# Attention steps between dense products, issued in runs of one kind and head

## The chip, the cores and the metric

The kernel runs on one core of a Trainium2 chip. The metric is the device time of one execution in microseconds (us); the output is compared with the reference. A core has TensorE (PE, matmuls; its weight loads, PEld, overlap them), VectorE (DVE), ScalarE (ACT), GpSimd (POOL), SyncE (SP, which here issues transfers) and 16 DMA engines.

## The reference

One layer of a decoder trunk: 512 tokens, 1024 features, 16 heads of 64, all in float32.

```python
hn = rms_norm(x, norm_g)
proj = hn @ w_in                      # queries, keys, values; six forget logits; gates of the FoX heads
q, k = rms_norm(q, q_gain), rms_norm(k, k_gain)          # per head
o_moba = moba_attention(...)          # heads 0-3: linear position bias; two blocks of 256, so all past keys
o_fox = forgetting_attention(...)     # heads 4-9: logits plus a cumulated log-sigmoid of the forget logits
o_dil = dilated_attention(...)        # heads 10-15: three dilated windows, mixed by their denominators
y = concatenate([rms_norm(o_moba, g), rms_norm(o_fox, g) * sigmoid(gate), rms_norm(o_dil, g)])
x = x + y @ w_out
x = x + square(relu(rms_norm(x, mlp_norm) @ w_up)) @ w_down
```

All attention is causal softmax attention over 512 keys with a bias that differs by kind of head.

## The kernel before

**Dense products.** Every float32 operand is split into two float32r parts, high and low, and a product is three matmuls (high by high, high by low, low by high) into one of four accumulator banks ("acc"). `Stream` loads weight pieces [128, n] with SyncE's queue and splits them: ScalarE writes the high part (L95 or L98), VectorE the low part (L96 or L99), two pieces ahead of their use. `product` yields after each triple of matmuls (L202).

**The phases.** First the input projection in nine chunks, tokens on the output's partitions: queries and keys of four heads (512 columns), their values (256; 262 for the third, with the forget logits), and so on, at last the gates (384). Each has eight pieces for each of four token tiles, 32 triples. Then the output projection with features on the partitions, in four parts: first the row tiles of the MoBA and dilated heads for both halves of the columns (`OUT_ORDER[:2]`, 20 triples each), then those of the FoX heads (12 each). Then the MLP. Heads are worked on in the order MoBA, dilated, FoX; "head 15" below is the last in this order, and heads 10 to 15 are FoX.

**Attention in steps.** While the dense triples of the input projection and of the first two parts of the output projection are issued, steps of attention are put between them. All steps write to four further banks ("m"), which are used in turn; a step can't begin before what the step four banks earlier wrote has been read.

- `stack` (two a head; L423): four transposes that put queries, then keys, with features on the partitions; ScalarE copies them out (L425), and behind the keys two DMAs on ScalarE's queue (L429, L430) make a copy of them with both parts changed over ("stk2").
- `s` (four a head, one for each query tile; L442): two matmuls of 128 to 512 columns, the second with the changed-over keys; FoX heads add a mask (L447). VectorE adds the bias and finds the minimum (L454), ScalarE takes the exponential (L456).
- `pt` (three a head; L469): four, three and three transposes of the probabilities, split by ScalarE (L475) and VectorE (L476).
- `av` (two a head, four matmuls each, one bank for both; L493): probabilities times values; ScalarE copies the result (L498).
- `o` (one a head; L508): four transposes, VectorE's sum (L510) and GpSimd's division (L517). After the last head of a group, `group_norm` follows: ScalarE's squares (L533), a root on VectorE, and the scaling (L540 with the gate, or L544).
- `y` (four a group; L550): transposes of a group's result, split by ScalarE (L553) and VectorE (L554); the output projection reads all four.
- `root`, `norm` (normalisation of queries and keys) and `sig` (the gates' sigmoid) have no work on TensorE; `f` accumulates the forget logits.

**Who goes when.** TensorE's instructions run in program order, and this order comes from a small planner. Each step names the steps it needs and a lag for each (`LAG`, in us of the planner's own clock, which counts a full triple as 0.654 and a step by `COST`). After each triple `attend` adds to a credit (1.2 for 512 columns, in proportion for fewer; 2.75 in the output projection; never over 3.0). As long as the credit is at least 1.0, the first step in the list (oldest head first) all of whose needs are old enough is issued; it costs 1.0 of credit, or 0.25 if it has no work on TensorE. At the start of the output projection `attend_until` issues, without regard to credit or lags, what is still owed of the dilated heads up to their last `o`, and then the four `y` of their group (`y1`). Just then the buffers of the input projection are given up, and four loads of 512 KB fetch the residual into that space on SyncE's queue (L651). Before the third part of the output projection the four `y` of the FoX heads (`y2`) must be done.

Of the kernel before, what the change touches and what calls it, by code (L numbers as in the profile page):

```python
# [27 lines left out]
BIG = 1.0e30  # L28
# [6 lines left out]
# Heads in the order in which they are worked on: MoBA, dilated, FoX. A group is its range in that  # L35
# order and the first row tile of its part of the output projection.
# [4 lines left out]
# Column chunks of the input projection, in the order in which they are computed.  # L41
# [5 lines left out]
def chunk_columns(kind, i):  # L47
    """Columns (first, how many) of four heads' queries and keys, of four heads' values (FoX's
    forget logits behind the third), or of FoX's output gates."""
    if kind == "qk":  # L50
        return [(m * D + DH * h, DH) for m in range(2) for h in HEADS[4 * i : 4 * i + 4]]
    if kind == "v":
        forget = [(3 * D, NFOX)] if i == 2 else []
        return [(2 * D + DH * h, DH) for h in HEADS[4 * i : 4 * i + 4]] + forget
    return [(3 * D + NFOX, NFOX * DH)]


class Stream:
    """Weights as [128, n] pieces: raw from DRAM, then split into two float32r parts whose sum is
    the float32 weight (times a per-row gain where one is given)."""  # L60
# [51 lines left out]
def hymba_block(ctx: ExitStack, tc: tile.TileContext, a, out):  # L112
# [4 lines left out]
    small = ctx.enter_context(tc.tile_pool(name="small", bufs=2))  # L117
# [15 lines left out]
    pieces, in_first = [], []  # L133

    def group(first, size, alone=0):
        """Pieces from `first` on that follow one another in DRAM are loaded together, up to `size`."""
        i = first + alone
        while i < len(pieces):
            n = 1
            while n < size and i + n < len(pieces) and pieces[i + n][1] == pieces[i][1] + n:  # L140
                n += 1
            pieces[i][2] = n
            i += n
# [31 lines left out]
    def product(first, ks, operands, banks_n, done, G=2):  # L175
        """One chunk: four accumulators over the pieces `ks`, three passes for each product of
        split operands. Yields after each (piece, accumulator)."""
# [7 lines left out]
        if first == 0:  # L185
            # The very first piece: one pass over all accumulators after another, as parts arrive.
            wh, wl = w.take(0)
            acc = [bank("acc") for _ in range(banks_n)]
            for m in (0, 2, 1):
                for b in range(banks_n):  # L190
                    pairs, view = operands(ks[0], b, wh, wl)
                    lhs, rhs = pairs[m]
                    nc.tensor.matmul(view(acc[b]), lhsT=lhs, rhs=rhs, start=(m == 0), stop=False)
            order = [(k, b) for k, b in order if k > 0]
# [14 lines left out]
    def rsqrt(y, v, n, t=None):  # L209
        """y = v ** -0.5 for positive v: a first guess from the exponent's bits, then Newton."""  # L210
# [17 lines left out]
    # the first use of ScalarE's tables, before there is data to wait for  # L228
    warm = small.tile([P, 1], F32, name="warm", bufs=1)
    nc.scalar.activation(warm, ones[:, :1], AF.Ln)  # L230
    # and TensorE's clock, which only a busy TensorE raises
# [13 lines left out]
    for k in range(NK):  # L245
# [9 lines left out]
        # Sum of squares over this core's rows of features, one column for each token.  # L255
# [15 lines left out]
    # mean(x^2) + eps for each token, eps times that, and the reciprocal root.  # L271
# [102 lines left out]
    def forget():  # L374
        # log sigmoid(f) = min(f, 0) - log(1 + exp(-|f|))
# [18 lines left out]
    def gate():  # L394
        # ScalarE changes its tables for this one: behind the last exponentials
        tc.keep_in_program_order(nc.scalar.activation(gsig, gsig, AF.Sigmoid))

# [16 lines left out]
    def stack_step(h, which):  # L414
        def f():
# [10 lines left out]
            if which == 1:  # L426
                # the same keys with their two parts changed over
# [33 lines left out]
    # Blocks (key tile, query tile) of the transposed probabilities, by accumulator bank.  # L461
# [95 lines left out]
    # A step goes between two dense products once what it needs was issued long enough before it  # L557
    # (microseconds of TensorE's work), the oldest head first, so that TensorE does not wait.
    LAG = {"qk": 2, "root": 3, "zero": 0.0, "each": 2.5, "v": 2.5, "f": 5, "stack": 5.5, "s": 3.5, "pt": 3, "av": 3, "free": 1, "cum": 7, "norm": 9}
    COST = {"stack": 0.25, "s": 0.3, "pt": 0.4, "av": 0.6, "o": 0.43, "y": 0.22, "f": 0.43, "root": 0.0, "norm": 0.0, "sig": 0.0}  # L560
    steps = []
# [54 lines left out]
    def attend(rate, cost):  # L616
        """After a dense product that holds TensorE for `cost`: attention steps, at most `rate` each."""
# [3 lines left out]
        while credit >= 1.0:  # L621
# [3 lines left out]
            issue(s)  # L625
            credit -= 1.0 if COST[s[0][0]] else WEIGHT

# [80 lines left out]
    p2.close()  # L708

    def x2_stats():  # L710
        # each row the same: the reciprocal root mean square of every token
# [54 lines left out]
def bias_tables():  # L766
    """Minus the position terms of the logits of the ALiBi heads, which depend on shapes alone:
    slope * distance, minus the log of how many dilated branches hold the key, BIG where none does.
    Column u of row p is the distance p + 384 - u."""
# [13 lines left out]
def tiles_of(m, width):  # L783
    """[rows, columns] as [column chunk][row in tile][row tile][column]."""
# [38 lines left out]
```

## Time and profile before

| | |
|---|---|
| median of three runs | 650.38 us (650.24 to 651.02) |
| span of the profiled execution, first to last instruction | 649.9 us |
| TensorE busy in it | 640.5 us |
| VectorE busy | 385.4 us |
| ScalarE busy | 299.1 us |
| GpSimd busy | 91.6 us |
| DMA | 68.40 MB |

The profiled execution's own time is known as its span; the runs were timed without a profile, and their median lies 0.5 us over it. Busy time of TensorE counts pipelined matmuls by modelled ends, so a matmul's real cost is read from one start to the next, or from the pieces of the chain of waits, which don't overlap.

### The profile page before, as it was taken

Reading aid. Unit: us, or ns where it says so; the run is one execution under the profiler, and the core shown is the slowest. Engines: PE = TensorE matmul, PEld = TensorE weight load, DVE = VectorE, ACT = ScalarE, POOL = GpSimd, SP = SyncE. Lnnn points to the kernel's source line nnn. Section 1 sums busy time; section 2 is a strip of 40 time slices with the busy share of each in tenths; the row PEclk is TensorE's granted clock in tenths of the full one; section 3 lists DMA queues with packets and bytes.
Section 4 is the critical chain, followed back from the end, with each engine's and each line's share of the span. In section 5 each row is a group of like instructions: output and inputs, shape, how many; then the busy total and the mean of one; then the engine's idle time right before and its main releaser. Section 6 shows DMA issues by size and latency. Waiting matters only on the chain.

```text
span 649.9 us, 9018 instructions
## 1 busy us (share of the span) xinstructions
PE 640.5 (99%) x3294; PEld 544.1 (84%) x3294; DVE 385.4 (59%) x771; ACT 299.1 (46%) x615; POOL 91.6 (14%) x97
## 2 busy tenths in 40 slices
PE   8999999999999999999999999999999999999997
PEld 6798898898899988887888888888888888888886
DVE  6794696796598646778954544266324544433531
ACT  7467776776777666454332322233222333223310
POOL 4300210111020100024220200022000211000100
PEclk9999999999999999999999999999999999999999
DMA  8435234244322551223133332233323233223311
GB/s 305 149 97 148 81 93 106 81 137 122 84 62 87 153 189 40 97 98 119 44 130 99 97 97 98 97 98 96 99 97 98 73 122 98 97 91 105 94 68 66
DMA packets 24044, 68.40 MB, mean 105 GB/s; under 512 B 3114, under 2 KB 4666, under 8 KB 24000
## 3 DMA queue, kind: packets, MB, share of 16 engines
q1 hardware_dynamic: 18224, 57.84, 27.3%
q10 hardware_dynamic: 4432, 5.77, 3.8%
q0 software_dynamic: 1344, 4.22, 2.5%
q8 instruction: 26, 0.43, 0.3%
q14 instruction: 18, 0.15, 0.1%
HBM read 61.51 MB, written 2.11 MB: 98 GB/s over the span
## 4 chain that ended last, share of the span: by engine, by line
PE 90%; DVE 4%; DMA 3%; ACT 1%; issue 1%; SPq 0%; POOL 0%; ACTq 0%; DVEq 0%
PE acc L202 80%; PE m L442 3%; PE m L493 2%; PE m L469 2%; DMA wraw<-in_w_in 2%; PE m L423 1%; DMA stk<-stk 1%; DVE ptl L476 1%; PE m L508 1%; DVE wlo L96 1%; PE m L550 0%; DVE osum L510 0%; DVE m L454 0%; ACT xh L250 0%; DVE qksq L261 0%
## 5 line engine op out<-in xcount | busy, mean ns | idle before, releaser
L96 DVE TENSOR_TENSOR wlo<-wraw,whi 128x512 fp32r<-128x512 f32 (+3 forms) x136 | 85.4, 634 | 93.0 <-ACT whi L95 90.4
L95 ACT CAST whi<-wraw 128x512 fp32r<-128x512 f32 (+3 forms) x135 | 75.5, 567 | 121.7 <-PE acc L202 117.6
L98 ACT ACTIVATE whi<-wraw,gains 128x512 fp32r<-128x512 f32 x80 | 57.2, 724 | 101.2 <-PE acc L202 101.2
L202 PE MATMUL acc<-whi,xh 128*128 128x512 f32 (+3 forms) x284 | 103.5, 365 | 0.3 <-DVE vs L358 0.2
L99 DVE SCALAR_TENSOR_TENSOR wlo<-wraw,gains,whi 128x512 fp32r<-128x512 f32 x80 | 61.0, 774 | 70.1 <-ACT whi L98 70.0
L202 PE MATMUL acc<-zh,whi 128*128 128x512 f32 x256 | 100.8, 394 | 0.7 <-issue 0.7
L202 PE MATMUL acc<-hl,whi 128*128 128x512 f32 x256 | 100.9, 394 | 0.0
L202 PE MATMUL acc<-zl,whi 128*128 128x512 f32 x256 | 100.8, 394 | 0.0
L202 PE MATMUL acc<-hh,whi 128*128 128x512 f32 x256 | 100.4, 392 | 0.0
L202 PE MATMUL acc<-zh,wlo 128*128 128x512 f32 x256 | 99.4, 388 | 0.0
L202 PE MATMUL acc<-hh,wlo 128*128 128x512 f32 x256 | 99.3, 388 | 0.0
L202 PE MATMUL acc<-wlo,xh 128*128 128x512 f32 (+3 forms) x284 | 95.5, 336 | 0.5 <-DVE wlo L96 0.5
L202 PE MATMUL acc<-whi,xl 128*128 128x512 f32 (+3 forms) x284 | 95.7, 337 | 0.0
L731 POOL TENSOR_TENSOR sq<-relu 128x512 f32<-128x512 f32 x32 | 38.2, 1196 | 267.0 <-DVE relu L729 266.2
L202 PEld LDWEIGHTS acc<-zh,whi 128*128 128x128 f32 x256 | 48.1, 188 | 12.5 <-issue 1.3
L202 PEld LDWEIGHTS acc<-whi,xl 128*128 128x128 f32 x284 | 53.6, 189 | 5.2
L202 PEld LDWEIGHTS acc<-hh,whi 128*128 128x128 f32 x256 | 48.1, 188 | 11.2
L202 PEld LDWEIGHTS acc<-hh,wlo 128*128 128x128 f32 x256 | 48.1, 188 | 10.8
L202 PEld LDWEIGHTS acc<-zh,wlo 128*128 128x128 f32 x256 | 48.1, 188 | 10.8
L202 PEld LDWEIGHTS acc<-wlo,xh 128*128 128x128 f32 x284 | 54.0, 190 | 3.2 <-DVE wlo L96 1.0
L202 PEld LDWEIGHTS acc<-whi,xh 128*128 128x128 f32 x284 | 53.7, 189 | 3.4 <-DVE vs L358 0.5
L202 PEld LDWEIGHTS acc<-zl,whi 128*128 128x128 f32 x256 | 48.1, 188 | 9.8 <-issue 0.2
(144 smaller groups left out, 906.1 us busy)
## 6 DMA issues: line engine op xcount, KB each, us to landing
wraw<-in_w_up SPq DMA_DIRECT2D x32, 512.0 KB, 4.0
wraw<-in_w_down SPq DMA_DIRECT2D x32, 512.0 KB, 3.4
wraw<-in_w_in SPq DMA_DIRECT2D x21, 512.0 KB, 3.9
stk<-stk ACTq DMA_DIRECT2D x32, 128.0 KB, 2.4
wraw<-in_w_out SPq DMA_DIRECT2D x6, 512.0 KB, 4.0
alibi<-in_alibi POOLq DMA_DIRECT2D x10, 256.0 KB, 3.5
x<-in_xT SPq DMA_DIRECT2D x4, 512.0 KB, 7.1
xraw<-in_xT SPq DMA_DIRECT2D x7, 256.0 KB, 6.6
```

The lines of the kernel that those rows point to most:

```text
L95: nc.scalar.copy(hi, raw)
L96: nc.vector.tensor_tensor(lo, raw, hi.bitcast(F32), op=ALU.subtract)
L98: nc.scalar.activation(hi, raw, AF.Copy, scale=gain)
L99: nc.vector.scalar_tensor_tensor(lo, raw, gain, hi.bitcast(F32), op0=ALU.mult, op1=ALU.subtract)
L202: nc.tensor.matmul(dst, lhsT=lhs, rhs=rhs, start=(k == 0 and m == 0), stop=(k == n - 1 and m == 2))
L423: nc.tensor.transpose(out=ps[:, t * P : (t + 1) * P].bitcast(F32R), in_=src, identity=identr)
L442: nc.tensor.matmul(ps[:, :n], lhsT=st[0][:, i * P : (i + 1) * P], rhs=st[m][:, :n], start=(m == 1), stop=(m == 2 and h < FOX0),)
L469: nc.tensor.transpose(out=ps[:, n * P : (n + 1) * P], in_=st["p"][i][:, j * P : (j + 1) * P], identity=ident)
L476: nc.vector.tensor_tensor(lo, ps[:, :n], hi.bitcast(F32), op=ALU.subtract)
L493: nc.tensor.matmul(ot[:, j * P :], lhsT=v, rhs=p, start=(half == 0 and j == 0), stop=(half == 1 and j == 3))
L508: nc.tensor.transpose(out=ps[:, i * P : (i + 1) * P], in_=st["ots"][:, i * P : (i + 1) * P], identity=ident)
L731: nc.gpsimd.tensor_tensor(sq, z, z, op=ALU.mult)
```

## The change

A step that the planner picks is no longer issued alone. Steps of the same kind and head with the next numbers are issued directly behind it, without asking for credit or for their needs, up to a multiple of a number by kind (`CHAIN`): both stacks, scores in pairs, all three transposes of probabilities, both products with the values, all four transposes of a group. Each takes its credit, which may so fall below zero. `attend_until` is as it was. Needs, lags and costs are the same, and so is each step's work. Comments were dropped from the file too.

```diff
     COST = {"stack": 0.25, "s": 0.3, "pt": 0.4, "av": 0.6, "o": 0.43, "y": 0.22, "f": 0.43, "root": 0.0, "norm": 0.0, "sig": 0.0}
+    CHAIN = {"stack": 2, "s": 2, "pt": 3, "av": 2, "y": 4}
     steps = []
...
             s = next((s for s in steps if eligible(s)), None)
             if s is None:
                 return
-            issue(s)
-            credit -= 1.0 if COST[s[0][0]] else WEIGHT
+            kind, h, n = s[0]
+            while s is not None:
+                issue(s)
+                credit -= 1.0 if COST[kind] else WEIGHT
+                n += 1
+                s = None if n % CHAIN.get(kind, 1) == 0 else next((x for x in steps if x[0] == (kind, h, n)), None)
```

## Rows read from the trace of the kernel before

**Rows 1.** The profile's first page: span, busy time of the engines (share of the span, instructions), and the shares of the chain of waits by engine.

```profile
span 649.9 us, 9018 instructions
...
PE 640.5 (99%) x3294; PEld 544.1 (84%) x3294; DVE 385.4 (59%) x771; ACT 299.1 (46%) x615; POOL 91.6 (14%) x97
...
PE 90%; DVE 4%; DMA 3%; ACT 1%; issue 1%; SPq 0%; POOL 0%; ACTq 0%; DVEq 0%
```

**Rows 2.** Busy time of each engine in two stretches (us from the span's start, length; busy us and instructions of PE, PEld, DVE, ACT, POOL; granted clock; DMA share; GB/s): the last value chunk, and the first two parts of the output projection.

```profile
185.40:204.50 19.10, 19.10 (x155) 18.63 (x154) 17.73 (x56) 14.42 (x39) 2.78 (x4) 1.00 0.21 57
...
233.70:276.60 42.90, 41.63 (x228) 35.04 (x227) 29.00 (x65) 24.67 (x53) 2.46 (x4) 1.00 0.35 111
```

**Rows 3.** The chain of waits from 48 to 110 us in order of time (start us, us, what; instructions of a line that follow one another are one piece): steps alone and in runs, and the dense triples ("x3" of L202) behind them.

```profile
48.46 0.98 PE m L423 x12
49.44 0.76 PE acc L202 x3
50.20 0.29 PE m L423 x4
50.50 0.75 PE acc L202 x3
...
55.40 0.81 PE m L442 x6
...
58.05 0.17 PE m L442 x2
58.22 0.75 PE acc L202 x3
58.97 0.23 PE m L442 x2
...
59.90 0.35 PE m L442 x2
...
60.93 0.44 PE m L469 x4
61.37 0.69 PE acc L202 x3
...
66.42 0.59 PE m L493 x4
67.01 0.74 PE acc L202 x3
...
73.89 0.33 PE m L469 x3
...
80.39 1.09 PE m L469 x10
...
97.45 1.23 PE m L493 x8
```

**Rows 4.** The timeline around the start of the output projection (start us, us, engine, line, operation, out<-in, form, count; in brackets idle time before it and what ended it): the last triple of the gate chunk ends where the first row begins.

```profile
233.66 0.60 PE L508 MATMUL m<-ident,ots 128*128 128x128 f32 x4
...
233.85 1.92 SPq L651 DMA_DIRECT2D x<-in_xT  x4
...
238.19 0.46 PE L423 MATMUL m<-identr,qks 128*128 128x128 f32 x4
...
239.81 0.61 ACTq L430 DMA_DIRECT2D stk<-stk  x1
...
245.46 0.31 PE L442 MATMUL m<-stk,stk 128*128 128x128 f32 x1
...
246.99 0.30 PE L442 MATMUL m<-stk,stk 128*128 128x128 f32 x1 [1.22 <-DMA stk<-stk]
```

**Rows 5.** The same timeline: the four y1 steps and the product behind them, the transposes of head 14's probabilities and VectorE's reading of them, the last scores of head 15 and ScalarE's reading of them.

```profile
234.09 1.96 PE L550 MATMUL m<-ident,o 128*128 128x128 f32 x12
...
235.80 0.48 PE L202 MATMUL acc<-y0h,whi 128*128 128x512 f32 x1
...
243.31 1.25 PE L469 MATMUL m<-ident,p 128*128 128x128 f32 x10
...
244.71 1.61 DVE L476 TENSOR_TENSOR ptl<-m,pth 128x512 fp32r<-128x512 f32 x3
...
248.73 0.68 PE L442 MATMUL m<-stk,stk 128*128 128x512 f32 x2
...
250.30 0.69 ACT L456 ACTIVATE p<-m,mn 128x512 f32<-128x512 f32 x1
```

**Rows 6.** The timeline of single engines and the chain's piece (fifth row) around the second and third part of the output projection: o of head 15, its group's norm, the y2 steps, their splits and the first matmuls that read them.

```profile
262.44 0.60 PE L508 MATMUL m<-ident,ots 128*128 128x128 f32 x4
...
272.50 1.14 PE L550 MATMUL m<-ident,o 128*128 128x128 f32 x9
...
276.81 0.39 PE L202 MATMUL acc<-y2l,whi 128*128 128x512 f32 x1
...
263.04 9.63 PE acc L202 x42
...
270.02 2.21 DVE L540 SCALAR_TENSOR_TENSOR o<-o,orr,gsig 128x384 f32<-128x384 f32 x4
...
274.00 1.94 DVE L554 TENSOR_TENSOR y2l<-m,y2h 128x384 fp32r<-128x384 f32 x4
...
273.03 1.24 ACT L553 CAST y2h<-m 128x384 fp32r<-128x384 f32 x3 [2.55 <-PE m L550]
```

## The prediction, made before the change was run

> **What bounds the kernel now.** I read the totals first, then the busy time by stage, then the chain of waits piece by piece, then the timeline around the places where TensorE waits. The totals and the chain [rows 1] are to show one thing: TensorE is busy 640.5 of 649.9 us and makes up 90% of the chain. So time can be won only where a TensorE instruction itself takes longer than it must, or in the few microseconds in which TensorE waits. The stages [rows 2] show the granted clock, 1.00, so the higher of its two levels, 2.4 GHz, and where another engine is near its own limit: VectorE is busy 17.73 of 19.10 us in the last value chunk, but 29.00 of 42.90 in the first half of the output projection. The pieces of the chain [rows 3] price an attention step alone and in a run, and the timelines [rows 4 to 6] show the waits.
>
> The span is 649.9 us and the median of the runs 650.38, so 0.5 us lie around the span. Nothing in the change touches what lies around it, so the sum is made as a difference and put on the median.
>
> **What the change does to the order.** I followed the planner's loop product by product with its own constants (LAG, COST, RATE, the widths 512, 256, 262 and 384). Attention now interrupts the dense products 89 times, before 151: the runs of kind s fall from 52 to 27, pt from 34 to 16, stack from 28 to 12, av from 24 to 16, y from 7 to 3; o stays at 16. Nothing is computed more or less. Credit may go below zero after a run, so the steps per product stay the same on average, but attention falls behind: at the end of the gate chunk the old order has finished the second product of head 12, the new one has not begun that head's transposes.
>
> **Step 1, TensorE's own time.** One triple of a dense product takes 0.69 to 0.70 us. I add to each step what the triple behind it takes above 0.69 [rows 3]. Transposes of probabilities: 0.44 for four, 0.33 for three; the triple behind is not longer in the chain. Three steps apart: 0.44 + 0.33 + 0.33 = 1.10; in one run of ten (0.109 each): 1.09. Scores: 0.17 + 0.06 for the first (its triple takes 0.75), 0.23, 0.35, together 0.81; the run of the same three: 0.81. Probabilities times values: 0.59 + 0.05 each, 1.28 for two; the run of eight takes 1.23, and with the same 0.05 behind it 1.28. Stacks: 0.29 + 0.06 = 0.35 alone; the run of twelve takes 0.98 + 0.06, 0.347 a step. The longer triple follows a short matmul, and in a run another step meets it instead. So a saved interruption is worth 0 to 0.02 us; 62 of them are worth 0 to 1.2 us, and I take 0.005 each, **-0.3**, since the scores, over a third of them, show no difference at all.
>
> **Step 2, the wait for the swapped keys of head 15.** The one large wait of the stretch: the first score matmul of head 15 starts at 245.46, the second needs the changed-over copy, whose last half is issued at 239.81, and starts at 246.99 [rows 4]. A matmul of that size passes in 0.06, so 1.47 us are lost. That copy shares the queues' engines with four loads of the residual, issued from 233.85 on, right after the gate chunk ends at 233.66. In the new order the stretch reads: y1 (four), product, pt of head 12, product, both stacks of 15, product, four scores of 14, product, av of 12, two products, pt of 13, product, o of 12, scores of 15. With the prices of step 1 the stacks end 12 x 0.109 + 0.70 + 1.09 + 0.70 + 0.64 = 4.4 us after the gate chunk, plus some 0.4 for banks (step 4): the 4.8 of before (238.5), so I let the copy land where it does now, 13.3 after the gate chunk. Behind the stacks come five products (3.5), four scores (0.17 + 0.06 + 0.23 + 0.35 and, in proportion to its columns, 0.46: 1.27, and 0.34 for their four masks at half of 0.17 each), av (1.28), pt (1.09) and o (0.44): 7.9 us, against the 7.0 from the end of the second stack (238.5) to 245.5. The swapped keys are then wanted at about 12.7. What is left of the wait is 0.6 by this count, and less by the longer first triples (0.05 each, five of them); I take 0.4, so **-1.1**, bounds -1.5 (all of it goes) and 0 (the loads push the copy back as far as the order moves it).
>
> **Step 3, the last transposes before the second half of the output projection.** Now o of head 15 starts at 262.44, fourteen products later (9.63) come three y2 steps at 272.50, one product, the fourth, three products, and at 276.81 the first matmul that reads y2's low part, one matmul (0.23) behind the first that reads its high part [rows 6]. VectorE finishes the last low part at 275.94, so 0.87 us early. In the new order head 15 is later: two products before the end of the first chunk it has done o of 14, and o of 15 comes after six products of the second; the fourteen of the norm's lag then end with the chunk, and all four y2 steps stand right before the first product that reads them. All of the cover is gone. From the start of y2: TensorE wants the low part 4 x 0.33 + 0.23 = 1.54 us later. ScalarE's first copy starts 0.53 after y2 starts, three of them take 1.24, so the fourth ends at 0.53 + 4 x 0.41 = 2.2, and VectorE's last subtraction takes 0.49 more (1.94 for four): 2.7. If an addition to the residual or a weight split stands among the subtractions, as it does now, it is 3.44 (275.94 minus 272.50). So a wait of 1.1 to 1.9 (2.7 or 3.44 less 1.54) arises, and up to 0.7 more if additions to the residual push back the gated norm, which now ends 272.23, only 0.3 before y2 starts. I take **+1.7**, bounds +1.1 and +2.6. Its cover could come only from work behind it on TensorE, which cannot overtake.
>
> **Step 4, accumulator banks.** All steps turn over four banks. The y1 run takes four at once behind steps whose results VectorE still reads: 1.71 us from 234.09 to 235.80 where 12 x 0.109 = 1.31 would do [rows 3, 5], 0.4 lost. In the new order y1 stands behind the scores of head 13, whose last two banks it needs 2.0 to 2.1 us after they were begun; a last score step is read out 2.26 after it begins (248.73 to 250.99). That wait halves: **-0.2**. A run of pt gives its first bank back 2.0 us after its start (243.31; three subtractions take 1.61 from 244.71 on). By the prices of step 1 the new order comes back to the same bank within 2.5 us at ten places other than the y1 run's own, before at four, all in the first half of the output projection: the three steps of pt 12 behind y1 (2.0 to 2.1), the second stack of 15 behind pt 12 (2.2), the scores of 15 behind pt 13 and o (2.1 to 2.2), the scores of 14 and av 12 among themselves (2.0 to 2.3). Most just fit. I take **+0.5**, bounds 0 and 10 x 0.4 = +4.0, nearer the low end because a run of ten transposes passes at the full rate now. The Trainium skill (Perfetto Trace Analysis, Matmuls) says that independent groups should rotate through different banks, so that the reading of one overlaps the matmuls of the next. That speaks against runs; the y1 run agrees, the run of ten does not wait.
>
> Weight splits are hidden by their lead of two pieces; in the narrow value chunks, where VectorE is busiest, pt already came as runs of three. I cost them at 0; without that cover each late piece costs a VectorE instruction, about 0.6.
>
> Sum: -0.3 - 1.1 + 1.7 - 0.2 + 0.5 = +0.6: 651.0 us.
>
> **The rivals.** Slower through banks: without the bank term the sum is -0.3 - 1.1 + 1.7 - 0.2 = +0.1; if five of the ten places cost the 0.4 of y1, it is +2.1, 652.5. It decides from four places on (1.6). For it speak the y1 run and that most places have a slack of 0.1 or so; against it, runs of pt that wait for nothing. Chance 0.20. Slower through y2 alone, at its upper bound of 2.6: the sum is +1.5, 651.9. For it: the norm's end just 0.3 ahead of y2 now. Against: it needs VectorE in the worst order. Chance 0.10. Faster through the waits: the copy's wait goes whole (-1.5), y2 costs its least (+1.1), banks nothing, a saved interruption its 0.02 (-1.2), and y1 -0.2: that is -1.8, 648.6. Against it: four terms at their ends. Chance 0.12. The change does more than is priced here, since each interruption has a fixed price: at the 0.06 of the first triples above it is 62 x 0.06 = 3.7 us in place of 0.3, the sum is -2.8, 647.6. The chain's pieces speak against it: a run pays as much as its parts. Chance 0.05. The Trainium skill (Perfetto Trace Analysis, Matmul Optimizations) says that matmuls should run back to back in batches because the engine's power follows its utilization; in the trace the clock is full in both stages [rows 2], single steps and all, so by that batches have nothing to win here.
>
> **The numbers.** The forecast has 0.53. A measurement of this kernel can tell about 0.2%, 1.3 us. Within it: 0.53; faster 0.12 + 0.05 = 0.17; slower 0.20 + 0.10 = 0.30. The range reaches from just inside the waits' rival, 648.7, to just above the banks' rival, 653.0; about 0.15 stays outside.
>
> **What would show it.** Step 1: pieces of ten transposes at 1.09 and pairs of av at 1.23, and the sum of TensorE's time without waits the same. Step 2: the wait for the swapped keys under 0.5. Step 3: a gap of over 1 us at the first y2 matmul. Step 4: runs of y, s or stack longer than their rows here. It is wrong if a stretch before the gate chunk's end is over 1 us shorter or longer, or if the other engines' order shifts so that weight splits come late.

## The result, and the profile after

The changed kernel takes 656.38 us (median of four runs, 655.95 to 657.35), the kernel before beside it 650.54 (650.24 to 651.02): a ratio of 1.009 [1.0075, 1.0104]. It is 5.8 us slower. The prediction said 651.0 with a range up to 653.0; it was wrong, and none of its rivals was large enough.

The totals of the changed kernel's first page, to set beside [rows 1]: the same instructions, TensorE busy 0.9 us longer, the span 4.2 us longer. So the time went into waits of TensorE.

```profile
span 654.1 us, 9018 instructions
...
PE 641.4 (98%) x3294; PEld 544.8 (83%) x3294; DVE 384.3 (59%) x771; ACT 298.4 (46%) x615; POOL 91.9 (14%) x97
```

The list of TensorE's waits in the changed kernel (what waited, for whom: us in total, times, longest). Most were not there before, where this list held for these stretches the swapped keys with 1.2 us and 0.2 for `vs`.

```profile
PE acc L202 <- DVE y2l L554: 1.2, 1, 1.2
PE acc L202 <- DVE vs L358: 1.1, 2, 0.9
...
PE acc L202 <- ACT y2h L553: 0.8, 1, 0.8
...
PE m L550 <- DVE y1l L554: 0.7, 1, 0.7
...
PE m L442 <- DVE ptl L476: 0.3, 1, 0.3
PE m L442 <- ACT p L456: 0.3, 1, 0.3
PE m L442 <- DMA stk<-stk: 0.3, 1, 0.3
```

This list counts only the time in which the array stood empty. What a wait costs is read better from one matmul's start to the next one's, less the usual distance of that pair of forms. Taken so, after the first 40 us and without 0.83 (before) and 0.88 (after) that both kernels lose at the start of the MLP:

| place (us in the changed kernel's trace) | waits for | before | after |
|---|---|---|---|
| scores, 129.7 to 177.2 | not named | 0 | 0.40 |
| first product behind the third value chunk, 148.6 in before | not named | 0.23 | 0 |
| scores behind `o` of head 9, 195.9 | bank, VectorE's `ptl` | 0 | 0.60 |
| scores, 201.5 | bank, ScalarE's `p` | 0 | 0.48 |
| first products of the gate chunk, 205.1 to 207.9 (208.45 in before) | accumulator, VectorE's `vs` | 0.34 | 1.62 |
| first scores of a head, 224.4 | swapped keys | 0 | 0.44 |
| y1 and the stack behind it, 232.3 | bank, ScalarE's `p` | 0.21 | 1.02 |
| first scores of head 15, 245.46 in before | swapped keys | 1.39 | 0 |
| y2 and the first products that read it, 278.1 | ScalarE, VectorE | 0 | 2.52 |
| sum | | 2.17 | 7.08 |

The kernel before so loses 0.34 at the gate chunk's first products too. Its chain of waits goes over VectorE's reading `vs` there, up to the product that starts at 208.88:

```profile
208.43 0.40 DVE vs L358
```

The difference is 4.9, the spans differ by 4.2. The rest, some 0.7 us, is put down to the 62 saved interruptions, about 0.01 each; no run measures it by itself.

One thing about before must be put right. In every run here of which both are known, time and span lie some 1.8 us apart (655.95 and 654.1 above; 650.39 and 648.6, 657.35 and 655.5 in others). So the profiled execution of before, with its span of 649.9, took some 651.7, not 650.4. The median execution is 1.2 us shorter, and what it lacks is, by two other traces, the wait for head 15's swapped keys. A kernel with the same order on TensorE (n_before, below) has that wait in its profiled execution, 651.05 us (first line), and its median is 649.91. A second one (b_y2late, below), with the same order up to the y2 steps, was profiled in an execution at its median (652.16 and 652.30), and there the two score matmuls run without a wait (second line).

```profile
246.34 0.30 PE L442 MATMUL m<-stk,stk 128*128 128x128 f32 x1 [1.04 <-DMA stk<-stk]
```

```profile
245.51 0.42 PE L442 MATMUL m<-stk,stk 128*128 128x128 f32 x2
```

So against the median the new waits are 7.08 less 0.78, 6.3, less the 0.7: 5.6, where 5.4 (the profiled execution, 655.95) to 5.8 (the median) were measured.

**y2.** The timeline of the changed kernel around the y2 steps, all engines:

```profile
275.52 1.67 DVE L540 SCALAR_TENSOR_TENSOR o<-o,orr,gsig 128x384 f32<-128x384 f32 x3
...
276.94 1.47 PE L550 MATMUL m<-ident,o 128*128 128x128 f32 x12
277.10 1.88 DVE L680 TENSOR_TENSOR x<-acc,x 128x512 f32<-128x512 f32 x3
277.54 1.60 ACT L553 CAST y2h<-m 128x384 fp32r<-128x384 f32 x4
278.90 1.94 DVE L554 TENSOR_TENSOR y2l<-m,y2h 128x384 fp32r<-128x384 f32 x4
279.19 0.50 PE L202 MATMUL acc<-y2h,whi 128*128 128x512 f32 x1 [0.78 <-ACT y2h L553]
...
280.90 0.50 PE L202 MATMUL acc<-y2l,whi 128*128 128x512 f32 x1 [1.20 <-DVE y2l L554]
```

The four transposes stand right before the product that reads them. Three additions to the residual (L680) stand on VectorE ahead of the low parts. In [rows 6] the low parts were done 0.87 us before they were read.

**The hand-over from the last value chunk to the gate chunk.** This is what the prediction priced at nothing; 1.62 us are lost there, 0.34 before. Single engines' timelines, the links of one chain in order:

```profile
198.63 0.86 POOL L517 TENSOR_TENSOR o<-osum,rden 128x256 f32<-128x256 f32 x1 [8.65 <-DVE osum L510]
...
199.53 0.53 ACT L533 ACTIVATE ots<-o 128x384 f32<-128x384 f32 x1 [2.42 <-POOL o L517]
...
201.69 0.17 DVE L536 TENSOR_SCALAR ov<-oss 128x4 f32<-128x4 f32 x1 [1.48 <-ACT ots L533]
...
204.50 1.40 DVE L544 TENSOR_SCALAR o<-o,orr 128x384 f32<-128x384 f32 x4
205.82 0.48 DVE L358 SCALAR_TENSOR_TENSOR vs<-acc,rx,vs 128x256 fp32r<-128x256 f32 x1
...
206.35 0.45 PE L202 MATMUL acc<-whi,xh 128*128 128x384 f32 x1 [0.89 <-DVE vs L358]
```

Head 9 is the last of its group, so its `o` brings the group's norm with it. ScalarE stands 2.42 us in front of the norm's squares until GpSimd has divided; VectorE stands 1.48 us in front of the norm's root until ScalarE has squared. Both engines work in program order, so whatever was issued later stands behind: the exponentials of the scores on ScalarE, the readings `vs` on VectorE that give the value chunk's accumulators back. TensorE arrives at the gate chunk and finds one accumulator unread.

### The profile page after: what moved, and what is told of

The parts are those of the page before. It is cut to its first block, busy times and chain, and to the rows that moved or that the text cites. A ratio compares the mean times of both kernels' runs of the same rounds, so it can differ in the third digit from the quotient of the medians.

```text
span 654.1 us, 9018 instructions
## 1 busy us (share of the span) xinstructions
PE 641.4 (98%) x3294; PEld 544.8 (83%) x3294; DVE 384.3 (59%) x771; ACT 298.4 (46%) x615; POOL 91.9 (14%) x97
## 4 chain that ended last, share of the span: by engine, by line
PE 56%; DVE 0%; issue 0%; DVEq 0%
PE acc L202 56%; DVE y2l L554 0%; PE m L720 0%; DVE x L755 0%; DVEq L826 0%
## 5 line engine op out<-in xcount | busy, mean ns | idle before, releaser
L202 PE MATMUL acc<-zh,whi 128*128 128x512 f32 x256 | 101.3, 396 | 0.7 <-issue 0.7
L202 PE MATMUL acc<-whi,xh 128*128 128x512 f32 (+3 forms) x284 | 99.9, 352 | 1.1 <-DVE vs L358 1.1
L202 PE MATMUL acc<-hh,whi 128*128 128x512 f32 x256 | 100.9, 394 | 0.0
L202 PE MATMUL acc<-hh,wlo 128*128 128x512 f32 x256 | 100.4, 392 | 0.0
L202 PE MATMUL acc<-zh,wlo 128*128 128x512 f32 x256 | 100.3, 392 | 0.0
L202 PE MATMUL acc<-zl,whi 128*128 128x512 f32 x256 | 99.4, 388 | 0.0
L202 PE MATMUL acc<-hl,whi 128*128 128x512 f32 x256 | 99.3, 388 | 0.0
L202 PE MATMUL acc<-wlo,xh 128*128 128x512 f32 (+3 forms) x284 | 95.4, 336 | 0.7 <-DVE wlo L96 0.7
L202 PE MATMUL acc<-whi,xl 128*128 128x512 f32 (+3 forms) x284 | 95.5, 336 | 0.0
L202 PEld LDWEIGHTS acc<-whi,xh 128*128 128x128 f32 x284 | 53.6, 189 | 6.0 <-DVE vs L358 1.9
L202 PEld LDWEIGHTS acc<-wlo,xh 128*128 128x128 f32 x284 | 53.8, 189 | 5.1 <-DVE wlo L96 1.1
L202 PEld LDWEIGHTS acc<-whi,xl 128*128 128x128 f32 x284 | 53.6, 189 | 5.3
L202 PEld LDWEIGHTS acc<-hh,wlo 128*128 128x128 f32 x256 | 48.0, 188 | 11.2
L202 PEld LDWEIGHTS acc<-zh,wlo 128*128 128x128 f32 x256 | 48.0, 188 | 11.2
L202 PEld LDWEIGHTS acc<-zh,whi 128*128 128x128 f32 x256 | 48.1, 188 | 11.0 <-issue 1.4
L202 PEld LDWEIGHTS acc<-zl,whi 128*128 128x128 f32 x256 | 48.1, 188 | 10.8 <-issue 0.2
L202 PEld LDWEIGHTS acc<-hl,whi 128*128 128x128 f32 x256 | 48.1, 188 | 10.8
```

The lines of the kernel that those rows point to most:

```text
L202: nc.tensor.matmul(dst, lhsT=lhs, rhs=rhs, start=(k == 0 and m == 0), stop=(k == n - 1 and m == 2))
```

## The experiments

Times are medians; "before" is the kernel before on the same chip. A wait is told as the excess of a start over the usual distance, as in the table.

**Which stage loses.** Runs only in the output projection (e2_only_out), only in the input projection (e3_only_in), only in the 512-column chunks (e4_wide):

```diff
-                s = None if n % CHAIN.get(kind, 1) == 0 else next(...)
+                s = None if n % CHAIN.get(kind, 1) == 0 or rate < 2 else next(...)      # e2_only_out
+                s = None if n % CHAIN.get(kind, 1) == 0 or rate > 2 else next(...)      # e3_only_in
+                s = None if n % CHAIN.get(kind, 1) == 0 or rate != 1.2 else next(...)   # e4_wide
```

> Runs only in the output projection, single steps in the input projection as before. The y2 steps are a run of four with four products behind them. Theory (late attention and VectorE in the fourth value chunk): nothing of either is left, so within 0.7 us of the kernel before. Rival (bank waits of runs, which the prediction saw in the first half of the output projection): 1 to 2 us over it.

> Runs only in the input projection, single steps in the output projection. Attention is as late as in the changed kernel; by the planner's loop y2 comes behind the last product again. Theory: all of the loss, 655.7 to 657. Rival (bank waits of runs in the output projection): 1 to 2 us less than the changed kernel, 654.5 to 655.5.

> Runs only in the chunks of 512 columns, single steps in value and gate chunks and in the output projection; 111 interruptions. Three y2 steps get one product of cover, the fourth none. Theory: the waits of the fourth value chunk go (about 3 us of the loss) and 1.5 to 2.5 us in front of the first y2 product stay: 652 to 653.5. Rival (each run costs alike): two thirds of the runs that the change makes are left, so two thirds of 5.8: 654.4.

Measured against 650.32: e2_only_out 650.56, ratio 1.0002 [0.9993, 1.0012]; e3_only_in 656.95, 1.0102 [1.0085, 1.0118]; e4_wide 657.00, 1.0098 [1.0083, 1.0113]. The output projection's runs cost nothing, the input projection's all of it, though y1 and y2, where part of it is lost, stand in the output projection. e4_wide was to be cheaper and was not: with no run in the value and gate chunks it still waits there (0.84 at 202 for a bank, ScalarE's `p`, and 0.35 at 205 for an accumulator), 2.24 at y2, and 1.0 at 95.7 for an accumulator that the changed kernel gets in time. So a hand-over can come late without a run standing at it: what the runs before it did to attention's schedule is enough.

**More attention per product.** The rate 1.3 instead of 1.2, with runs (e1_rate13) and in the kernel before (b_rate13):

```diff
-    RATE, RATE2 = 1.2, 2.75
+    RATE, RATE2 = 1.3, 2.75
```

> The changed kernel with one number altered: the credit per dense product is 1.3 instead of 1.2, so attention is no longer behind; runs stay (91 interruptions). By the planner's loop the y2 steps come four products before the second half of the output projection instead of none. Theory (runs cost nothing, being late costs): the 2.5 us in front of the first y2 product go, and the waits of the fourth value chunk (3.4 us in all there) change but stay in part: 652 to 654. Rival (each run costs through its banks, wherever it stands): 656 or more, since there are as many runs.

> The kernel before with a rate of 1.3 in place of 1.2, the same raise that took the wait at y2 out of the changed kernel but cost it 6.2 us up to the last value chunk. If that loss was the rate's (attention issued faster than VectorE and ScalarE read it out), it is here too: 653 to 656. If it was the runs' (three steps at once beside dense products), single steps take the raise: 649.3 to 651.0, with no wait over 0.5 us before the output projection and none for the swapped keys of head 15.

e1_rate13 took 655.66 against 650.32, ratio 1.0078 [1.0063, 1.0093], between the theory's 652 to 654 and the rival's 656. The wait at y2 is gone, since attention is early enough again for four products to stand between the transposes and their reader. But the input projection loses elsewhere what y2 gives back: its last value chunk begins at 191.51, in the kernel before at 185.35. These 6.2 us are not all loss, as the expectation of b_rate13 above and that of n_gate below take them: at the higher rate more of attention stands ahead of that chunk, and in b_rate13, which loses nothing, it begins at 189.35. At least the other 2.2 are lost. The largest wait is again for an accumulator at a chunk's beginning, here one of the third value chunk's with the forget logits (1.31 us up to 152.90, for VectorE's `fl`).

b_rate13 took 650.44 against 650.34, ratio 0.9997 [0.9988, 1.0007]: single steps take the higher rate at no cost in the sum. So the loss needs the runs.

**Each kind of run alone:**

```diff
-    CHAIN = {"stack": 2, "s": 2, "pt": 3, "av": 2, "y": 4}
+    CHAIN = {"stack": 2}      # k_stack;  {"s": 2}: k_s;  {"pt": 3}: k_pt;  {"av": 2}: k_av
```

> Runs for one kind alone: the two stacks of a head. 140 interruptions, y2 with its four products of cover, the keys of head 15 swapped before the output projection begins, so ahead of the loads of the residual. Theory A (bursts on VectorE and ScalarE): two copies on ScalarE, none on VectorE, so 650 to 651. Theory B (being late): no loss either, 649.5 to 650.5. A fixed saving for each run that is made, as in the rival of the prediction (0.06): 650.3 less 0.7.

> Runs for one kind alone: scores in pairs; all other steps singly. 121 interruptions. By the planner's loop attention is late, and y2 comes without any product behind it. Theory A (what costs is the burst of results that a run hands to VectorE and ScalarE, here two reductions and two exponentials at once, and the lost cover of y2): 653.5 to 656, with waits before scores or weight splits in the input projection and 2 to 2.5 us at y2. Theory B (only being late costs): 652.5 to 653, all of it at y2.

> Runs for one kind alone: the three transposes of probabilities. 135 interruptions; three of the y2 steps get one product of cover, the fourth none. Theory A (bursts: three copies and three subtractions at once): 652.5 to 655, part of it in the input projection. Theory B (only being late costs): 652, all of it at y2.

> Runs of kind av alone (CHAIN with av: 2; 24 interruptions become 16). If the loss were a sum over kinds, the three runs of one kind so far (+10.1, +10.4, -0.4) would leave av at -14 to make the +5.8 of all together, which cannot be. If the loss is where the hand-overs of other engines happen to fall, av alone, whose run changes few of them, gives 649.8 to 652, and whatever it loses stands as two or three waits of TensorE over 0.4 us at y1, at y2 or in the last value or gate chunk.

| runs of | us (before) | ratio | waits over 0.6 us |
|---|---|---|---|
| stack | 649.85 (650.27) | 0.9993 [0.9984, 1.0003] | none |
| s | 660.33 (650.27) | 1.0155 [1.0140, 1.0170] | 0.63, 0.73, 2.81, y2 2.4 |
| pt | 660.66 (650.27) | 1.0156 [1.0141, 1.0172] | 2.44, 1.32, 0.99, y1 0.99, y2 2.2 |
| av | 654.36 (650.34) | 1.0051 [1.0035, 1.0067] | 0.83, 1.68, 0.64, y1 0.82 |

Only stack came as expected; s, pt and av lie 4.3, 5.7 and 2.4 us above the upper ends of their forecasts. Alone, s and pt cost nearly twice what all kinds cost together. Part of that is the clock behind their waits: in their profiled executions it falls to half for 3.4 us, twice in k_s (from 240.2 and 284.6 on, some 3.4 us of TensorE's time) and once in k_pt (from 283.7 on, 1.7). Less these, 6.7 and 8.7 us are left, still more than all kinds together. The cost is no sum over the runs. Each setting makes another schedule, and each schedule strikes other queues. In k_s ScalarE's sigmoid of the gates, with a table load on either side, gets in front of the exponentials that TensorE needs (timelines of ScalarE and TensorE):

```profile
235.03 1.28 ACT L396 ACT_TABLE_LOAD   x1
236.32 1.49 ACT L396 ACTIVATE gsig<-gsig 128x1536 f32<-128x1536 f32 x1
237.82 1.28 ACT L456 ACT_TABLE_LOAD   x1
...
239.63 0.98 PE L493 MATMUL m<-pth,vs 128*128 128x512 f32 x4 [2.65 <-ACT p L456]
```

In k_pt it is the copy of swapped keys, in a chunk where no load of the residual is in the way:

```profile
169.29 0.59 PE L442 MATMUL m<-stk,stk 128*128 128x128 f32 x3 [2.28 <-DMA stk<-stk]
```

In k_av it is the same place as in the changed kernel, but the work that stands before `vs` on VectorE is another, the normalisation of queries and keys (L346) and the low parts of a run of transposes:

```profile
204.92 1.28 DVE L346 TENSOR_TENSOR qks<-qkraw,qks 128x512 fp32r<-128x512 f32 x2
206.12 1.02 DVE L476 TENSOR_TENSOR ptl<-m,pth 128x384 fp32r<-128x384 f32 x2
207.06 0.47 DVE L358 SCALAR_TENSOR_TENSOR vs<-acc,rx,vs 128x256 fp32r<-128x256 f32 x1
...
207.59 0.44 PE L202 MATMUL acc<-whi,xh 128*128 128x384 f32 x1 [1.54 <-DVE vs L358]
```

**The price of y2's cover.** The kernel before with a longer lag for y2 alone, so that its transposes stand right before their reader:

```diff
-            step(("y", g, t), partial(y_transpose, g, t), [(..., "norm")])
+            step(("y", g, t), partial(y_transpose, g, t), [(..., "norm" if g == 1 else "late")])   # "late": 13
```

> The kernel before with one number altered: the four y2 steps must be 13 and not 9 of the planner's microseconds behind o of head 15, so that they stand right before the product that reads them, but the group's norm is done well before. It prices the lost cover by itself. Prediction's step 3: 1.1 to 1.9 us over the kernel before. In the changed kernel 2.5 us stand there; if all of that were lost cover and not a late norm, 2.5.

It took 652.30 against 650.27, ratio 1.0032 [1.0019, 1.0045]; the wait is 1.9. This is the upper end of step 3's 1.1 to 1.9. The low parts begin 1.32 us after the transposes (273.85), behind a weight split and one addition:

```profile
274.57 0.68 DVE L673 TENSOR_TENSOR x<-acc,x 128x512 f32<-128x512 f32 x1
275.17 1.94 DVE L554 TENSOR_TENSOR y2l<-m,y2h 128x384 fp32r<-128x384 f32 x4
```

In the changed kernel they begin 1.96 us after the transposes, behind the end of the norm's scaling and three additions. These 0.64 later are the rest of its 2.5.

**Is it VectorE's load?** The low parts of the weights of the last value and gate chunks on GpSimd, in the changed kernel (a_pool) and in the kernel before (b_pool):

```diff
-                nc.vector.tensor_tensor(lo, raw, hi.bitcast(F32), op=ALU.subtract)
+                (nc.gpsimd if i in self.lo_pool else nc.vector).tensor_tensor(...)   # lo_pool: pieces 56 to 71
```

> The changed kernel, with the low parts of the weights of the last value chunk and of the gate chunk (16 pieces; 420 and 601 ns each on VectorE, 8.2 us together) subtracted on GpSimd, which is mostly idle there. Theory: the 2.6 us of new waits between 195 and 208 us come from VectorE being late (it is busy 14.18 of the 15 us from 186 to 201, and 5.00 of 5.00 from 205 to 210); with 8.2 us less on it they fall under 0.7, and the time is 653.9 to 654.8 (about -2). Rival: VectorE was as full there before the change, the waits come from attention's hand-overs coming in lumps, on whichever engine; then the time is 655.5 or more, and waits stand there still or have moved on.

> The kernel before with the same 16 low parts on GpSimd. It had no wait over 0.35 us in these two chunks, so by both theories there is nothing to win: 650.0 to 650.8. Over 651 would say that GpSimd's longer subtraction (0.74 us for 256 columns by its other rows) delays the products, which would then count against the run above too.

a_pool took 658.84 against 650.34, ratio 1.0131 [1.0107, 1.0155]; b_pool 656.12, 1.0077 [1.0054, 1.0100]. a_pool's theory missed, and so did the expectation that the kernel before would not mind. The rival's bound, 655.5 or more, is met, but as the run takes some 2.5 us more than the changed kernel, it does not speak for the rival either. With 8 us less to do, VectorE gave the accumulators back later (in a_pool the second `vs` starts at 207.86, in the changed kernel at 205.82). The timelines of GpSimd and VectorE in b_pool show why:

```profile
203.72 1.02 POOL L97 TENSOR_TENSOR wlo<-wraw,whi 128x384 fp32r<-128x384 f32 x1 [2.21 <-ACT whi L96]
...
206.45 2.27 POOL L97 TENSOR_TENSOR wlo<-wraw,whi 128x384 fp32r<-128x384 f32 x2 [1.71 <-ACT whi L96]
```

```profile
203.53 0.16 DVE L219 SCALAR_TENSOR_TENSOR orr<-rs_t,orr 128x4 f32<-128x4 f32 x1
203.73 1.03 DVE L217 SCALAR_TENSOR_TENSOR rs_t<-orr,ov 128x4 f32<-128x4 f32 x1
...
206.04 2.90 DVE L545 TENSOR_SCALAR o<-o,orr 128x384 f32<-128x384 f32 x4
```

A step of the root on four numbers a partition, 0.16 us otherwise, takes 1.03 beside GpSimd's subtraction of 1.02; the four scalings of the norm take 2.90 in place of 1.40. TensorE waited 1.21 for `vs` and then 2.45 for `ptl`, and of b_pool's 5.8 us some 3.4 are the lower clock behind these waits (0.87, 0.50 and 0.95 in the 5 us from 205, 210 and 215 on). So load was the wrong word: what counts is when VectorE reaches one instruction, and this run shows how little it takes to delay that. It does not acquit VectorE's load by itself, as GpSimd disturbed it.

**The queue's order.** The norm of heads 4 to 9 is issued 12 us of the planner's clock later, in the gate chunk. TensorE's order stays, matmul by matmul. In the changed kernel (n_after) and in the kernel before (n_before):

```diff
-            if h + 1 == GROUPS[g][1]:
+            if h + 1 == GROUPS[g][1] and g != 1:
                 group_norm(g)
...
             attend(RATE * n / 512, TOKEN * n / 512)
+            if late_norm and clock > issued.get(("o", 9, 0), 1e9) + 12:      # late_norm = [1]
+                group_norm(late_norm.pop())
```

> The changed kernel with one thing moved: the norm of the group of heads 4 to 9 (ScalarE's squares, VectorE's root and scaling) is issued 12 us of the planner's clock behind the last o of the group, in the gate chunk, not directly behind it. TensorE's order is the same, matmul by matmul. Theory (the queues' order: squares and root stand waiting in front of the readings that free the banks): of the 2.6 us of waits between 195 and 208 us at least 1.5 go, y1 and y2 stay, and the time is 653.9 to 655.0. Rival (attention's readings are late in any case, being wanted three at a time): the waits stay within 0.5 us, 655.9 or more.

> The kernel before with the same norm moved in the same way. ScalarE and VectorE stood waiting there as well (1.76 and 1.10 us), but TensorE did not, so by both theories nothing changes: 650.0 to 650.8. If it is faster by over 1 us, TensorE lost time there that I don't see in its waits.

n_after took 654.96 against 650.37, ratio 1.0069 [1.0054, 1.0084]; n_before 649.91, 0.9991 [0.9982, 1.0001]. The theory holds: all waits from 201 to 208 us are gone, 2.1 in the table, and the one for the swapped keys at 224 too; y1 and y2 stay. The second `vs` ends 3.2 us earlier and no product of the gate chunk waits. VectorE, then TensorE:

```profile
202.63 0.48 DVE L358 SCALAR_TENSOR_TENSOR vs<-acc,rx,vs 128x256 fp32r<-128x256 f32 x1 [0.78 <-ACT vs L357]
...
204.98 0.34 PE L202 MATMUL acc<-whi,xh 128*128 128x384 f32 x1
```

In n_before the 0.34 at the gate chunk's beginning goes too, which its expectation had overlooked; its median is 0.46 lower, just within the interval.

The median of n_after gives back only 1.4 of the 2.5 (1.25 when each kernel is set against the kernel before on its chip), since in this kernel's profiled execution the waits at y2 are followed by 3.4 us in which a matmul of 512 columns takes 0.43 instead of 0.23, the lower clock: eight of them, 1.6 us. The stretch behind y2 in n_after (start and end, length; busy us and count of PE, PEld, DVE, ACT, POOL; granted clock, DMA share, GB/s):

```profile
280.00:285.00 5.00, 5.00 (x18) 4.02 (x18) 0.00 (x0) 0.20 (x1) 0.00 (x0) 0.77 0.65 210
```

and in the changed kernel, where the same two waits (0.78 and 1.20) cost no clock:

```profile
280.00:285.00 5.00, 4.10 (x18) 3.44 (x19) 2.17 (x4) 0.00 (x0) 0.00 (x0) 1.00 0.42 113
```

**Both hand-overs.** n_after with a rate of 1.6 in the gate chunk, which puts two products between y2 and its reader (n_gate):

```diff
-            attend(RATE * n / 512, TOKEN * n / 512)
+            attend((1.6 if kind == "g" else RATE) * n / 512, TOKEN * n / 512)
```

> The changed kernel with the norm moved and, in the gate chunk alone, a rate of 1.6 in place of 1.2, so that attention catches up before the output projection and y2 gets two products (1.4 us) of cover. If the loss is these two hand-overs, the wait at y2 falls from 2.5 to about 1.1 and the time is 652.0 to 653.6. If a raise of the rate under runs brings new waits wherever it is made (6.2 us for the raise to 1.3 everywhere), they stand in the gate chunk and the time is 655 or more.

It took 652.60, ratio 1.0034 [1.0022, 1.0047], with 1.1 left at y2 and 0.8 at y1. The two places are 3.8 of the 5.8 us (3.6, each against the kernel before on its chip); the 1.1 at y2, the 0.8 at y1 and the 0.5 that is left at 195.8 are the largest parts of the rest.

**A version that beats both.** What had cost nothing, together: stack runs, the moved norm and the rate 1.3 (n_best); the same without the rate (s_norm).

```diff
+    CHAIN = {"stack": 2}      # and the norm moved, as in n_after
+    RATE, RATE2 = 1.3, 2.75   # n_best only
```

> What cost nothing so far, together: runs of kind stack alone (649.85 by itself), a rate of 1.3 (650.44 by itself on single steps), and the norm moved. Theory: each leaves TensorE's order free of new waits, and y2 keeps its cover; 649.0 to 650.3. Rival: the higher rate moves hand-overs onto one another as it did with all runs; over 651, with a wait of over 0.8 us before the output projection.

> Runs of kind stack alone and the norm of heads 4 to 9 moved, at the rate of 1.2: the last run without its raise of the rate. If the raise made its waits, none over 0.6 us is left and the time is the two parts' own, 649.0 to 650.2 (649.85 and 649.91 singly). If the moved norm made them, 651.5 or more.

n_best took 653.63 against 650.37, ratio 1.0048 [1.0033, 1.0063]: three harmless edits together cost 3.3 us, with waits of 1.26 at y1 (a bank, behind ScalarE's `p`), 0.91 (157.6), 0.71 (149.9) and 0.75 (246.5). s_norm took 649.25 against 650.63, ratio 0.998 [0.9971, 0.9989], faster than both kernels. So the raised rate, on top of the other two, made those waits. The whole list of TensorE's waits in s_norm has nothing left after the first 40 us but the MLP's start ("issue", 0.7):

```profile
PE acc L193 <- DVE xh L248: 2.1, 1, 2.1
PE acc L202 <- DVE wlo L96: 1.9, 2, 1.6
PE m L234 <- DVE ones L227: 1.0, 1, 1.0
PE acc L202 <- issue: 0.7, 1, 0.7
```

## Why the prediction was wrong

**What was right.** Step 1: a run pays as much as its parts. In the changed kernel ten transposes take 1.01 from their start to the next product's (first and second line), and that triple is 0.08 longer: 1.09, as in [rows 3].

```profile
208.49 1.25 PE L469 MATMUL m<-ident,p 128*128 128x128 f32 x10
209.50 0.42 PE L202 MATMUL acc<-whi,xh 128*128 128x384 f32 x1
```

An interruption saved is worth about 0.01 us rather than 0.005, inside the bounds. Step 3's mechanism was right. The Trainium skill (Perfetto Trace Analysis, Matmul Optimizations) wants matmuls in back-to-back batches because the engine's power follows its use. By that rule runs had nothing to give here: TensorE was back to back in single steps too, busy 99% of the span [rows 1] with the clock full [rows 2]. Longer runs of one kind brought no clock, only waits, two of which cost clock in n_after.

**By term,** in us, forecast and measured against the median: step 1 -0.3 and -0.7; step 2 -1.1 and 0; step 3 +1.7 and +2.5; y1 -0.2 and +0.8; all other banks, accumulators and swapped keys, step 4's +0.5 and its nothing for the rest, +3.0. The sum was +0.6 and comes to +5.6.

**Step 4 failed.** It counted banks that come back within 2.5 us, found such places only in the first half of the output projection and took +0.5. There the runs cost nothing (e2_only_out). All the cost of that kind lies earlier, in the input projection, where the step said nothing: 0.60 and 0.48 for banks, 1.62 (0.34 before) for accumulators, 0.40 among scores and 0.44 for swapped keys. It looked at how soon TensorE comes back to a bank, and took the reader's delay from single rows of the output projection (2.0 and 2.26 us). What set that delay at 201 to 208 us is what stood before the reading in the other engines' queues: GpSimd's division, then four squares, a root and four scalings (n_after). The paragraph on the weight splits saw that VectorE is nearly full in the last value chunk [rows 2], but asked only whether a split comes late for its product; after the first 40 us none did. The trace of before had the warning: ScalarE and VectorE stand 1.76 and 1.10 us in front of the same norm, and TensorE then waits 0.34 for `vs`. An idle engine that holds its queue was not looked for, as its idle time seemed free.

**Step 4, y1.** "That wait halves" was wrong: it grew from 0.4 (0.2 by the table's measure) to 0.87. The last two scores of head 13 stand as a pair one product ahead of it. The first three banks come back in time, the fourth, wanted 2.15 us after its score was begun (230.26), about as forecast, does not:

```profile
231.42 1.15 PE L550 MATMUL m<-ident,o 128*128 128x128 f32 x9
233.28 0.55 PE L550 MATMUL m<-ident,o 128*128 128x128 f32 x3 [0.71 <-DVE y1l L554]
```

The profile names VectorE's `y1l`, but what ends just then is ScalarE's exponential of the fourth score, 3.0 us after the score was begun where the step read 2.26. It starts as soon as VectorE has found the score's minimum (232.58), and that reading stood behind the low part of a weight; ScalarE itself came to it behind a copy of y1. The two engines' timelines (VectorE, then ScalarE):

```profile
231.16 0.75 DVE L99 SCALAR_TENSOR_TENSOR wlo<-wraw,gains,whi 128x512 fp32r<-128x512 f32 x1
231.83 0.69 DVE L454 CUSTOM_DVE_ANT_0 m<-m,ck 128x512 f32<-128x512 f32 x1
232.44 0.14 DVE L454 DVE_READ_ACCUMULATOR2_ANT mn<- 128x1 f32 x1
```

```profile
232.15 0.48 ACT L553 CAST y1h<-m 128x384 fp32r<-128x384 f32 x1
232.62 0.69 ACT L456 ACTIVATE p<-m,mn 128x512 f32<-128x512 f32 x1
```

Again it seems to be the queues in front of the readers, not the readers; no run takes this place apart.

**Step 3 was mis-sized:** +1.7 where 2.5 was measured. Its upper bound nearly came: the last low part ends 3.9 us after y2 starts (280.84 less 276.94), where the sum had 2.7 to 3.44, behind the end of the norm's scaling and three additions. Its 1.1 to 1.9 hold one addition or weight split at most; yet it had itself worked out that y2 now falls at the end of a chunk, and just there the accumulators are read out into additions. The rival "slower through y2 alone" had the right size for y2 (2.6), a chance of 0.10, and with its 651.9 still only a quarter of the loss.

**Step 2 was right in the trace and worth nothing in the median.** Head 15's swapped keys no longer wait. But by the traces of n_before and b_y2late that wait is not in the median run, which the prediction could have suspected: it put 0.5 us around the span, the difference of a long execution's span and a median.

**What was missing as a rival:** that attention, later and in lumps (the last value chunk begins 2.3 us earlier than before, 183.04 and 185.35, with steps still owed), meets every fixed hand-over of the kernel at another moment. Four kinds of runs gave -0.4, +4.0, +10.1 and +10.4 us, none of which the steps would have told. What stays open is why each of those schedules strikes just the places it does; only 201 to 208 us and y2 were taken apart by experiments, 4.6 of the 7.1 us in the table. Nor do the runs tell lateness from lumps: none makes all of attention as late with single steps.

## What to carry to other kernels

An interleaving of small steps with a long stream carries fixed hand-overs (accumulators at a chunk's change, operands of the next stage, a table switch), and an edit of its grain must be priced at each of them by the whole queue in front of the releasing instruction, not by the instruction's own duration. An engine that stands idle at the head of its queue, waiting for another, is the place to look: moving one such norm later won about 1.3 us in one order and took away a wait of 0.34 in the other. If a trace is one execution and the target a median, first find which waits of the trace the median does not have.

## What the runs showed of the hardware that was not expected

GpSimd can hold VectorE up: in b_pool a VectorE instruction of 0.16 us took 1.03, the length of the GpSimd subtraction that ran at that time, and four scalings took 2.90 instead of 1.40; in a_pool they took 2.21. The Trainium skill (SBUF — State Buffer, Who interferes with whom) says that the two share a port pair that one of them holds for a whole instruction, VectorE being affected where it has two inputs in that memory or runs in a two-port mode; by that, the trace agrees, with 1.03 against 1.02.

Short waits can cost the clock for longer than they last. After 2.65 us of waiting in k_s the granted clock is 0.66 on average over the 5 us from 240 on (first line); after waits of 1.21 and 2.45 in b_pool it is half, the lower level of 1.2 GHz, for 5 us in a row (second line; columns as in the stretches above):

```profile
240.00:245.00 5.00, 5.00 (x26) 4.43 (x25) 0.00 (x0) 2.85 (x8) 0.00 (x0) 0.66 0.05 19
```

```profile
210.00:215.00 5.00, 5.00 (x22) 4.71 (x22) 2.25 (x6) 1.07 (x2) 0.61 (x1) 0.50 0.22 88
```

The two waits at y2 show that it isn't certain: 0.78 and 1.20 us, one matmul apart, left the clock at 1.00 in the changed kernel's profile and took it to 0.77 in n_after's. The changed kernel's fourth run had a mean clock of 0.995 and took 657.35, 1.4 us over its first with 1.00; that run left no trace, so whether these waits did it is not known.
